# A hybrid DeltaNet and attention layer: inverses by rank-one updates on two engines, a bias table from 128 partitions, and new buffers in the second half

## The chip, the cores and the metric

The kernel runs on one core of a Trainium2 chip. A core has five engines that work side by side, each with its own instruction stream: TensorE (PE, matrix products into PSUM), VectorE (DVE), ScalarE (ACT), GpSimd (POOL) and SyncE (SP, which issues transfers). Transfers between DRAM and SBUF are issued from SP and from ACT and run on the core's DMA engines. The metric is the time of one execution on the device in microseconds; the median of three runs stands for a kernel. The profile comes from one more execution.

## The reference

The layer normalises x (2048 tokens by 1024), projects it by w_in, runs two token mixers side by side, and projects both back by w_out. This is its core, shortened:

```python
h = rms_norm(x, norm_w)
qkv_dn, z_dn, b_dn, a_dn, qkv_att, gate_att = split(h @ w_in)
# A: gated DeltaNet, 4 heads of 128, chunks of 64
q, k, v = split(silu(causal_depthwise_conv(qkv_dn, conv_w)))       # width 4
a_mat = tril_strict((beta * k) @ k.T * decay);  l_mat = a_mat + I   # per chunk, 64x64
u = solve(l_mat, beta * v);  w = solve(l_mat, beta * k * exp(gc))
# over the 32 chunks:  v_new = u - w @ S;  o = q_dec @ S + attn @ v_new
#                      S = S * g_last + k_tail.T @ v_new
y_dn = rms_norm(o) * silu(z_dn)
# B: dilated attention, 8 heads of 64, patterns (128,1), (512,4), (2048,16)
# scores + rel_bias[bucket(distance)], softmax; patterns weighed by their denominators
y_att = sum_p(weight_p * out_p) * silu(gate_att)
return x + concat(y_dn, y_att) @ w_out
```

All in float32. A large product is done as three: each operand is split into a high part (`wh`, `xh`, from ACT) and a low part (`wl`, `xl`, the remainder, from DVE), and high by high, low by high and high by low are summed in PSUM.

## The kernel before

Work stands in this order in the file, and a scheduler orders each engine's instructions by priorities (`tc.cur_priority`), so that the stages overlap.

1. **Projections of DeltaNet.** `conv_proj` (L460) makes q, k and v, 512 tokens by 128 channels at a time: 24 products `pj` (L206 to L208), scaled on DVE into `cu` (L474), the width-4 convolution as one ACT operation into `cy` (L476) and three DVE operations (L478), SiLU on ACT (L480) and a store to DRAM from ACT's queue (L481). `gate_proj` (L483) makes the attention's gate in the same manner. Their weights are 512 KB loads `wraw` (L187) into two buffers, split by ACT (L191) and DVE (L192).
2. **`stage1a`** (L501) forms the 64x64 matrices of the chunks (A) and the decays (E) and writes both to DRAM, in two halves of 16 chunks (`hf` 0 and 1).
3. **`inverse`** (L535) then inverts, per half, all 128 diagonal blocks of 32x32, one in each partition: the blocks come back from DRAM into `L`, ACT negates them, and for i = 1 to 31 DVE multiplies an i by i product (L545) and sums it along its rows into column i of `Tt` (L547). The inverse goes back over its place in A (L551), and a transposed copy goes to D (L552). Both writes, and later the loads of the weights, stand in SP's queue in the order of the schedule.
4. **Bias table** (L579 to L594): a one-hot product gives for 8 heads and 3 patterns a row of 256 biases, in 8 partitions. Three writes copy each row 64 times to `bs_d`, from which the attention later loads a skewed `bias` tile per head pair.
5. **`stage2`** (L606) prepares four chunks of a head pair: it loads kT, qT, vT, Qr, E, TT (A with its inverted blocks) and D0t (D) on SP's queue, and PE finishes the 64x64 inverse from the 32x32 blocks (L642), then forms the tiles of the delta rule (to L699). **`chain`** (L712) runs the rule chunk by chunk. **`dn_out`** (L741) loads `zs`, the gate of y_dn, scales and gates `o4` in place, and stores it to `y_d`. PE fills the time between with the projections of the attention (`proj_fill`, L886), whose operations carry the line L99, as do all that go through the file's helper.
6. **Attention and output projection.** From L1239 a table of steps (`at_step`, 12 steps to a head pair) calls a head pair's `load` (q, K, bias), `queries`, `keys`, `vload`, `scores`, `values` and its weighing by hand. `out_fill` (L1359) generates in the second half (steps from 48) the output projection's products `po`, that fill PE between them: `half_load` loads `yt` (y_dn) or `mt` (y_att), `half_split` splits it into `mh`, `wo_split` (L865) splits w_out, and `res_load` loads x or a stored partial sum into `res`. Buffers come from the pool `wo`, whose places are given out in the order of allocation.

## Time and profile before

| quantity | value |
|---|---|
| runs | 1434.2 us median of 3 (1432.68 to 1436.26) |
| profiled execution | 1434.53 us, of which the span of the trace is 1432.6 us |
| mean granted clock of PE | 0.988 |
| ACT busy | 47% of the span |
| DMA | 205.00 MB in 301154 packets, mean 143 GB/s |

The span is the time from the first to the last instruction in the trace; some 1.9 us of the execution lie around it. A row of a group names its line, engine, operation, tiles (out<-in), shape and count, then busy time and the mean of one in ns, and after the next bar the idle time of the engine just ahead of it and what ended that. A row of the timeline gives start, duration, engine and operation, with idle time and releaser in brackets. SPq and ACTq rows are issues of transfers. In the chain that ended last, a DMA row is the time in which a transfer was waited for.

### The profile page before, as it was taken

How to read it: one execution, taken by the hardware profiler on the slowest of the kernel's cores; microseconds unless marked ns; L12 is line 12 of the kernel's file. 1: busy time of each engine (PE TensorE's matmuls, PEld its weight loads, DVE VectorE, ACT ScalarE, POOL GpSimd, SP SyncE). 2: the span in 40 equal slices, each digit the busy share in tenths (PEclk: the TensorE clock that was granted, in tenths of full speed). 3: DMA queues.
4: the chain of work that ended last, by engine and by line, in shares of the span. 5: the costliest groups of instructions: out<-in, count | busy, mean ns of one | idle time of the engine just before them, and what ended most of it. 6: DMA issues, size and time to landing. Idle time of an engine off the chain costs nothing.

```text
span 1432.6 us, 28797 instructions
## 1 busy us (share of the span) xinstructions
PE 1376.4 (96%) x10262; PEld 1224.8 (85%) x10262; DVE 905.4 (63%) x2787; ACT 677.1 (47%) x1929; POOL 438.4 (31%) x507
## 2 busy tenths in 40 slices
PE   8999999999999997999999899999998989999998
PEld 7998777777777797999999889999997778888877
DVE  7535668799995365777777664634444645556465
ACT  5634436652221333444444376666565545555520
POOL 3000000000002113442332523565675275665500
PEclk9999999999999999999999999999999999999999
DMA  6563446763648646557553555274657474765664
GB/s 192 179 111 83 101 89 136 150 121 84 116 77 176 171 80 165 134 147 193 129 147 77 114 132 137 76 190 98 147 135 235 138 253 135 220 169 158 194 191 142
DMA packets 301154, 205.00 MB, mean 143 GB/s; under 512 B 149283, under 2 KB 271027, under 8 KB 300500
## 3 DMA queue, kind: packets, MB, share of 16 engines
q1 hardware_dynamic: 233924, 171.70, 48.6%
q10 hardware_dynamic: 67088, 31.47, 8.0%
q8 instruction: 81, 1.33, 0.4%
q14 instruction: 61, 0.50, 0.1%
HBM read 142.61 MB, written 60.50 MB: 142 GB/s over the span
## 4 chain that ended last, share of the span: by engine, by line
PE 66%; DVE 14%; DMA 9%; ACT 4%; issue 4%; SPq 1%; POOL 1%; ACTq 0%; DVEq 0%; POOLq 0%
PE pj L99 15%; PE po L99 9%; PE sc L99 6%; PE pz L99 5%; PE pv L99 4%; PE pj L206 4%; PE pj L207 4%; PE pj L208 4%; PE pt L99 4%; DVE cy L478 3%; DVE inv L545 2%; DMA kT<-cv 2%; PE C L719 2%; PE SU L725 2%; DVE inv L547 2%
## 5 line engine op out<-in xcount | busy, mean ns | idle before, releaser
L99 ACT ACTIVATE pr<-pr,ml 128x192 f32<-128x192 f32 (+2 forms) x384 | 156.8, 409 | 168.7 <-DVE ml L99 156.9
L99 PE MATMUL pj<-wh,xh 128*128 128x256 f32 (+1 forms) x776 | 228.2, 294 | 3.6 <-DVE t L99 2.3
L99 PE MATMUL pj<-wl,xh 128*128 128x256 f32 (+1 forms) x776 | 226.6, 292 | 0.0
L99 PE MATMUL pj<-wh,xl 128*128 128x256 f32 (+1 forms) x776 | 224.9, 290 | 0.0
L208 PE MATMUL pj<-xh,wl 128*128 128x512 f32 x512 | 203.6, 398 | 3.2 <-DVE wl L192 3.2
L206 PE MATMUL pj<-xh,wh 128*128 128x512 f32 x512 | 203.8, 398 | 1.4 <-ACT cy L480 1.2
L207 PE MATMUL pj<-xl,wh 128*128 128x512 f32 x512 | 203.0, 396 | 0.0
L99 PEld LDWEIGHTS pj<-wh,xh 128*128 128x128 f32 x776 | 147.6, 190 | 4.3 <-DVE t L99 2.7
L99 PEld LDWEIGHTS pj<-wl,xh 128*128 128x128 f32 x776 | 148.0, 191 | 0.6 <-issue 0.4
L99 PEld LDWEIGHTS pj<-wh,xl 128*128 128x128 f32 x776 | 147.7, 190 | 0.2
L99 DVE CUSTOM_DVE_ANT_0 pr<-sc,bias 128x192 f32<-128x192 f32 (+2 forms) x384 | 100.3, 307 | 74.3 <-PE sc L99 73.4
L208 PEld LDWEIGHTS pj<-xh,wl 128*128 128x128 f32 x512 | 96.5, 188 | 26.6 <-DVE wl L192 4.5
L206 PEld LDWEIGHTS pj<-xh,wh 128*128 128x128 f32 x512 | 96.6, 189 | 24.8 <-ACT cy L480 1.6
L478 DVE SCALAR_TENSOR_TENSOR cy<-cu,cw,cy 128x512 f32<-128x512 f32 x144 | 107.6, 749 | 15.9 <-ACT cy L476 14.4
L207 PEld LDWEIGHTS pj<-xl,wh 128*128 128x128 f32 x512 | 96.5, 188 | 22.0
L99 POOL COPY qz<-q 64x512 f32<-64x512 f32 x96 | 94.5, 984 | 57.8 <-PE sc L99 53.9
L662 POOL MEMSET at__4536<- 64x256 f32 x1 | 0.3, 306 | 354.5 <-PE pj L207 354.5
L99 DVE COPY pT<-pt 64x128 f32<-64x128 f32 (+2 forms) x220 | 69.4, 323 | 60.1 <-PE pt L99 56.8
L99 PE MATMUL po<-xh,mhh 128*128 128x512 f32 x212 | 89.6, 422 | 2.5 <-ACT mhh L99 2.5
L99 POOL TENSOR_TENSOR Fb<-Fb,op 128x256 f32<-128x256 f32 x84 | 70.6, 854 | 60.8 <-DMA Fb<-F 59.7
L99 PE MATMUL po<-xl,mhh 128*128 128x512 f32 x212 | 88.6, 418 | 0.0
L99 PE MATMUL po<-xh,mhl 128*128 128x512 f32 x212 | 88.4, 417 | 0.0
(365 smaller groups left out, 3169.8 us busy)
## 6 DMA issues: line engine op xcount, KB each, us to landing
wraw<-in_w_in SPq DMA_DIRECT2D x44, 512.0 KB, 7.0
cv<-cy ACTq DMA_DIRECT2D x48, 256.0 KB, 2.6
Fb<-F SPq DMA_DIRECT2D x64, 192.0 KB, 5.8
xr<-in_xT SPq DMA_DIRECT2D x32, 256.0 KB, 4.1
kT<-cv SPq DMA_DIRECT2D x32, 256.0 KB, 3.3
qk<-qs ACTq DMA_DIRECT2D x64, 128.0 KB, 3.6
res<-in_x SPq DMA_DIRECT2D x13, 512.0 KB, 5.3
V<-v_d SPq DMA_DIRECT2D x20, 256.0 KB, 6.2
```

Of the source, the lines that this page charges most:

```text
L99: i = f(*args, **kw)
L206: nc.tensor.matmul(ps, wh[:, k, c * P:(c + 1) * P], xh[tb][:, kt, :], start=kt == 0, stop=False)
L207: nc.tensor.matmul(ps, wh[:, k, c * P:(c + 1) * P], xl[tb][:, kt, :], start=False, stop=False)
L208: nc.tensor.matmul(ps, wl[:, k, c * P:(c + 1) * P], xh[tb][:, kt, :], start=False, stop=kt == KT - 1)
L478: nc.vector.scalar_tensor_tensor(y, u[:, i:i + 512], cw[:, ct, i:i + 1], y, op0=ALU.mult, op1=ALU.add)
L545: nc.vector.tensor_tensor(pr_[:, :i, :i], Tt[:, :i, :i], L[:, None, :i, i].to_broadcast([P, i, i]), op=ALU.mult)
L547: nc.vector.tensor_reduce(Tt[:, :i, i], pr_[:, :i, :i], axis=AX.X, op=ALU.add)
L662: nc.gpsimd.memset(at_[:CH, :, :CH], 0.0)
L719: nc.tensor.matmul(pc[:, s_], g["WQ"][:, u, s_], S0[:, s_], start=True, stop=True)
L725: nc.tensor.matmul(su[:, s_], g["Ks"][:, u, s_], VN, start=True, stop=True)
```

## The change

Of the whole diff (blank lines and unchanged parts are left out):

```diff
-    bs_d = dr.tile([8, 3, 64 * 256], F32, name="bs_d")
+    bs_d = dr.tile([3, 8, 64 * 256], F32, name="bs_d")
...
+        eng = (nc.vector, nc.gpsimd)[hf]
         nc.scalar.mul(L, L, -1.0)
-        nc.vector.memset(Tt, 0.0)
-        nc.vector.memset(Tt.rearrange("p c i -> p (c i)")[:, 0:1024:33], 1.0)
-        for i in range(1, 32):
-            nc.vector.tensor_tensor(pr_[:, :i, :i], Tt[:, :i, :i], L[:, None, :i, i].to_broadcast([P, i, i]),
-                                    op=ALU.mult)
-            nc.vector.tensor_reduce(Tt[:, :i, i], pr_[:, :i, :i], axis=AX.X, op=ALU.add)
+        eng.memset(Tt, 0.0)
+        eng.memset(Tt.rearrange("p c i -> p (c i)")[:, 0:1024:33], 1.0)
+        for j in range(31):
+            n, m = j + 1, 31 - j
+            eng.tensor_tensor(pr_[:, :n, :m], Tt[:, :n, j:j + 1].to_broadcast([P, n, m]),
+                              L[:, j:j + 1, n:].to_broadcast([P, n, m]), op=ALU.mult)
+            eng.tensor_tensor(Tt[:, :n, n:], Tt[:, :n, n:], pr_[:, :n, :m], op=ALU.add)
         D0 = pr_
-        nc.vector.tensor_copy(D0[:64], Tt[:64].rearrange("p c i -> p i c"))
+        eng.tensor_copy(D0[:64], Tt[:64].rearrange("p c i -> p i c"))
...
+    mid.tile([P, 512], F32, name="t0", bufs=2)
     rs0 = [mid.tile([P, 512], F32, name="big", bufs=3) for _ in range(2)]
...
+    rb16 = scr[:N_BUCKETS + 1, 1552:1680]
+    nc.vector.tensor_copy(rb16.rearrange("p (h c) -> p h c", h=8), rb[:, :, None].to_broadcast([N_BUCKETS + 1, 8, 16]))
+    bv = scr[:, :768].rearrange("p (a b) -> p a b", a=3)
...
-        nc.tensor.matmul(pb[:8, :n], rb, oh[:, i * 512:i * 512 + n], start=True, stop=True)
-    for i in range(3):
-        dma(dap(bs_d, i * 64 * 256, [[3 * 64 * 256, 8], [256, 64], [1, 256]]),
-            bv[:, i, None, :].to_broadcast([8, 64, 256]))
+        nc.tensor.matmul(pb[:, :n], rb16, oh[:, i * 512:i * 512 + n], start=True, stop=True)
+    def bias_out(i, after):
+        d = dma(dap(bs_d, i * 8 * 64 * 256, [[4 * 256, P], [256, 4], [1, 256]]),
+                bv[:, i, None, :].to_broadcast([P, 4, 256]))
+        tc.add_manual_dep(d.ins, after.ins.name, NOSYNC, reason="behind the loads of a group of chunks")
...
-    def stage2(pair, c0):
+    def stage2(pair, c0, dma2=dma):
...
-        dma(E, Es_d[hf][pair, cc:cc + 4].rearrange("u p i -> p u i"))
+        dma2(E, Es_d[hf][pair, cc:cc + 4].rearrange("u p i -> p u i"))
...
-            dma(TT[a:a + CH, :, a:a + CH], A_d[hf][pair, cc:cc + 4, a:a + CH].rearrange("u p i -> p u i"))
-            dma(D0[a:a + 32], dap(D0_d[hf], (m0 + s_) * 1024, [[32, 32], [2048, 4], [1, 32]]))
+            dma2(TT[a:a + CH, :, a:a + CH], A_d[hf][pair, cc:cc + 4, a:a + CH].rearrange("u p i -> p u i"))
+            dma2(D0[a:a + 32], dap(D0_d[hf], (m0 + s_) * 1024, [[32, 32], [2048, 4], [1, 32]]))
...
-        zs = dn.tile([P, 4, P], F32, name="zs", bufs=1)
+        zs = dn.tile([P, 4, P], F32, name="zs", bufs=2)
...
+            if c0 == 0:
+                tc.add_manual_dep(z.ins, last_D0[0].ins.name, NOSYNC, reason="behind the first preparations'")
...
-            nc.vector.scalar_tensor_tensor(g["o4"][:, u], g["o4"][:, u], f[:, 1, u:u + 1], zs[:, u],
+            nc.vector.scalar_tensor_tensor(zs[:, u], g["o4"][:, u], f[:, 1, u:u + 1], zs[:, u],
...
-                g["o4"][(1 - s_) * CH:(2 - s_) * CH])
+                zs[(1 - s_) * CH:(2 - s_) * CH])
...
-        G[p_] = at_prio("prep", stage2, p_, 0)
+        G[p_] = at_prio("prep", stage2, p_, 0, adma)
...
+        if c0 < 12:
+            at_prio("out", bias_out, c0 // 4, z)
...
     def w_out_load(k):
-        r = wp.tile([P, 4, 260], F32, name="wraw", bufs=2).rearrange("p a b -> p (a b)")[:, :1024]
+        if k == 2:
+            rs = [mid.tile([P, 512], F32, name="big", bufs=3) for _ in range(2)]
+        else:
+            rs = [wp.tile([P, 4, 260], F32, name="wraw", bufs=2).rearrange("p a b -> p (a b)")[:, :1024]]
...
-            at_step(b - 4, 1, g["load"])
+            at_step(*((b - 4, 1) if i < 4 else (b - 3, 0) if i == 4 else (b - 3, 2)), g["load"])
...
+    wo.tile([P, 512], F32, name="mt", bufs=2)
+    C1 = wo.tile([P, S], F32, name="C1")
+    loaded = {i: half_load(Q2[i], "dn", 4) for i in range(2)}
     RAW = [wo.tile([P, D], F32, name="res", bufs=3) for _ in range(2)]
-    C1 = wo.tile([P, S + 80], F32, name="C1")[:, :S]
-    loaded = {i: half_load(Q2[i], "dn", 4) for i in range(2)}
...
-        for k in range(4):
-            dma(RAW[k], w_out[(4 + k) * P:(5 + k) * P, :])
+        raws = {(0, 1): (raw_load, 0), (0, 2): (raw_load, 1), (0, 12): (raw_load, 2), (0, 22): (raw_load, 3)}
+        for k, at_ in enumerate(((0, 20), (1, 8), (1, 20), (2, 8))):
+            raws[at_] = (lambda k=k: wo_split(4 + k, RAW[k]),)
```

The inverse is now formed by 31 rank-one updates, of the first half on DVE and of the second on POOL. A step j multiplies column j of `Tt` by row j of `L` (a product of j + 1 by 31 - j) and adds it to the right. The bias table is laid out by pattern first, and each head's row stands in 16 partitions. Its three writes go one behind each of the first three groups of chunks. E, TT and D0t of the first two preparations go by ACT's queue (`adma`), the zs loads of the first group behind the last of these preparations' Qr loads. y_dn is written over `zs`, which has two buffers, instead of over `o4`. In the second half, the buffers of the pool `wo` are given out in another order (`mt`, `C1`, `yt`, `res`, `K1`), `mh` has one tile for both parts, w_out's third block is loaded early, into two `big` tiles that `wo_split` takes one by one, and its last four blocks are loaded and split at four places of the products each. The loads of q, K and bias of the head pair 4 stand two thirds of a step later (at the start of step b - 3), those of 5 to 7 at the end of that step.

SP's queue where the convolutions end and the second half's inverse comes back. `inv_2689` is L of the second half, loaded from `A1_71`; `A1_71<-inv`, `D01_75<-inv` are the writes of its result, `wraw` the weights of the gate, `big` the norms' rows. Before:

```order
L187 DMA wraw_3945<-in_w_in 128x4x256
L187 DMA wraw_4067<-in_w_in 128x4x256
L540 DMA inv_2689<-A1_71 64x32x32 x2
L551 DMA A0_70<-inv_2360 64x32x32 x2
L552 DMA D00_74<-inv_2361 64x1024
L187 DMA wraw_4073<-in_w_in 128x4x256
L187 DMA wraw_4204<-in_w_in 128x4x256
L187 DMA wraw_4210<-in_w_in 128x4x256
L187 DMA wraw_4332<-in_w_in 128x4x256
L551 DMA A1_71<-inv_2690 64x32x32 x2
L552 DMA D01_75<-inv_2691 64x1024
```

After:

```order
L540 DMA inv_2689<-A1_71 64x32x32 x2
L553 DMA A0_70<-inv_2360 64x32x32 x2
L554 DMA D00_74<-inv_2361 64x1024
L187 DMA wraw_3946<-in_w_in 128x4x256
L187 DMA wraw_4068<-in_w_in 128x4x256
L553 DMA A1_71<-inv_2690 64x32x32 x2
L554 DMA D01_75<-inv_2691 64x1024
L187 DMA wraw_4074<-in_w_in 128x4x256
L575 DMA big_3936<-rstd_d_69 128x512
L575 DMA big_3937<-rstd_d_69 128x512
L187 DMA wraw_4205<-in_w_in 128x4x256
L187 DMA wraw_4211<-in_w_in 128x4x256
```

The load of the blocks moved ahead of two weight loads, and the two writes of the result moved ahead of the four weight loads of the gate that they stood behind (`wraw_4073` is now `wraw_4074`).

SP's queue where the bias table is written (`bs_d`), among the loads of the second group's preparations. Before:

```order
L99 DMA wraw_7453<-in_w_in 128x4x256
L594 DMA bs_d_86<-K0_4460 8x64x256
L635 DMA TTz1_4474<-A0_70 64x4x64 x2
L636 DMA D0t_5102<-D00_74 32x4x32 x2
L594 DMA bs_d_86<-K0_4460 8x64x256 x2
L619 DMA qT_5089<-cv00_57 128x512
L629 DMA E2_5100<-Es0_72 128x4x64
L618 DMA kT_5088<-cv10_59 128x512
L620 DMA vT_4826<-cv21_62 128x512
```

After:

```order
L99 DMA wraw_7455<-in_w_in 128x4x256
L643 DMA TTz1_4473<-A0_70 64x4x64 x2
L601 DMA bs_d_86<-K0_4461 512x1x256
L644 DMA D0t_5102<-D00_74 32x4x32 x2
L627 DMA qT_5089<-cv00_57 128x512
L637 DMA E2_5100<-Es0_72 128x4x64
L626 DMA kT_5088<-cv10_59 128x512
L628 DMA vT_4825<-cv21_62 128x512
```

One of the three writes is left there, 512 rows from 128 partitions; the other two stand some 20 rows further on each.

SP's queue in the second half, at the loads of head pair 5 (`q1`, `K1`, `bias`) and of the next tile of x (`res<-in_x`). Before:

```order
L99 DMA V_13204<-v_d_84 128x4x128
L99 DMA q1_13237<-qk01_77 128x1024
L99 DMA K1_12654<-qk11_81 128x2048
L99 DMA bias_13240<-bs_d_86 64x3x192 x2
L99 DMA acc_d_104<-res_13001 128x1024
L99 DMA mx_d_103<-gt_13057 128x256
L99 DMA res_13318<-in_x 128x1024
L99 DMA V_13325<-v_d_84 128x4x128
```

After:

```order
L99 DMA V_13207<-v_d_84 128x4x128
L99 DMA acc_d_104<-res_13003 128x1024
L99 DMA mx_d_103<-gt_13061 128x256
L99 DMA res_13314<-in_x 128x1024
L99 DMA V_13321<-v_d_84 128x4x128
L99 DMA q1_13323<-qk01_77 128x1024
L99 DMA K1_12661<-qk11_81 128x2048
L99 DMA bias_13326<-bs_d_86 64x3x192 x2
```

The loads of q, K and bias moved behind the store of a partial sum, the load of x and a load of V.

More of the change, by code (lines that the diff above doesn't have):

```diff
@@ L780, in hybrid @@
         for p_ in range(2):
-            at_prio("out", dn_out, p_, c0, cur[p_])
+            z = at_prio("out", dn_out, p_, c0, cur[p_])
+        if c0 < 12:
+            at_prio("out", bias_out, c0 // 4, z)
     close(psD_g)
@@ L867, in wo_split @@
         if kt < 4:
-            nc.scalar.mul(wh, raw, dnw)
-            nc.vector.scalar_tensor_tensor(wl, raw, dnw, wh.bitcast(F32), op0=ALU.mult, op1=ALU.subtract)
+            for i, r in enumerate(raw):
+                n = r.shape[1]
+                h, l = wh[:, i * n:(i + 1) * n], wl[:, i * n:(i + 1) * n]
+                nc.scalar.mul(h, r, dnw)
+                nc.vector.scalar_tensor_tensor(l, r, dnw, h.bitcast(F32), op0=ALU.mult, op1=ALU.subtract)
         else:
@@ L881, in w_out_load @@
     def w_out_load(k):
-        r = wp.tile([P, 4, 260], F32, name="wraw", bufs=2).rearrange("p a b -> p (a b)")[:, :1024]
-        dma(r, w_out[k * P:(k + 1) * P, :])
-        return r
+        if k == 2:
+            rs = [mid.tile([P, 512], F32, name="big", bufs=3) for _ in range(2)]
+        else:
+            rs = [wp.tile([P, 4, 260], F32, name="wraw", bufs=2).rearrange("p a b -> p (a b)")[:, :1024]]
+        n = D // len(rs)
+        for i, r in enumerate(rs):
+            dma(r, w_out[k * P:(k + 1) * P, i * n:(i + 1) * n])
+        return rs
     def proj_fill():
@@ L917, in proj_fill @@
                     if o8 == 1:
-                        rs = [w_out_load(k) for k in range(2)]
+                        rs = [w_out_load(k) for k in range(3)]
                     if o8 == 4:
@@ L980, in load @@
                 dma(bias[s_ * CH:(s_ + 1) * CH],
[L981 removed]
+                    dap(bs_d, (2 * p + s_) * 64 * 256 + 63, [[255, CH], [8 * 64 * 256, 3], [1, 192]]))
             g["kc"] = {0: g["k1"].rearrange("p (c i) -> p c i", c=1)}
@@ L1312, in ring_mh @@
     def ring_mh():
-        return [wo.tile([P, 4, P], F32R, name="mh" + c, bufs=3) for c in "hl"]
+        t = wo.tile([P, 2, 4, P], F32R, name="mh", bufs=3)
+        return [t[:, 0], t[:, 1]]
     def res_load(tt, src, res=None):
@@ L1389, in split @@
                 if buf not in spare:
-                    t = wo.tile([P, S + (80 if buf == "C1" else 48)], F32R, name=buf)[:, :S]
+                    t = wo.tile([P, S + (0 if buf == "C1" else 150)], F32R, name=buf)[:, :S]
                     t = t.rearrange("p (a b k c) -> p a b k c", a=2, b=2, k=4)
@@ L1426, in out_fill @@
                     m += 1
-                    if nth < 2 and m in (8, 16):
-                        k = 2 * nth + m // 8 - 1
-                        wo_split(4 + k, RAW[k])
+                    if (nth, m) in raws:
+                        f, *args = raws.pop((nth, m))
+                        f(*args)
                     if m >= 3 * n and m % 3 == 0 and todo_:
```

20 lines of the change are left out of this document (11 added, 9 removed).

## The prediction, made before the changed kernel ran

> **What bounds the kernel now.** I read the page's first part, then the waits of PE, then windows with the granted clock.
>
> ```profile
> span 1432.6 us, 28797 instructions
> PE 1376.4 (96%) x10262; PEld 1224.8 (85%) x10262; DVE 905.4 (63%) x2787; ACT 677.1 (47%) x1929; POOL 438.4 (31%) x507
> ```
>
> PE is the bound. The change takes no matmul away, so all it can win lies in the 1432.6 - 1376.4 = 56.2 us in which PE is idle, and in what follows an idle stretch. The waits of PE (us in total, times, longest) say which those are:
>
> ```profile
> PE A L680 <- DMA vT<-cv: 6.6, 1, 6.6
> PE pv L99 <- DVE pT L99: 5.1, 2, 4.5
> PE sc L99 <- DVE ml L99: 4.3, 3, 2.3
> PE A L642 <- DMA D0t<-D: 4.2, 1, 4.2
> PE pv L99 <- DVE res L99: 3.7, 1, 3.7
> PE pj L208 <- DVE wl L192: 3.2, 3, 1.5
> PE po L99 <- DMA yt<-y_d: 1.8, 1, 1.8
> ...
> PE pj L206 <- ACT cy L480: 1.2, 1, 1.2
> ```
>
> A window behind the last-but-one of these (columns: stretch, length, PE, PEld, DVE, ACT, POOL busy with counts, granted clock, DMA share, GB/s) shows a second price:
>
> ```profile
> 1101.70:1105.10 3.40, 3.40 (x12) 3.21 (x11) 1.29 (x8) 1.26 (x5) 0.92 (x2) 0.50 0.54 188
> ```
>
> Behind the wait for yt (to 1099) the clock is 0.50 for 3.4 us. Work done in 3.4 us at half clock would take 1.7 us at full clock, so I put each wait of 1.8 us or more at its length and 1.6 us besides. By the Trainium skill (TensorE: Matmul & The Clock Gate, section Part 1: The HAM clock gate) the clock halves only after an idle window of about 3.4 us. The row has the half clock behind a wait of 1.8 us, so here the measurement decides. With that rule the term of yt below would be 1.6 us smaller, and nothing else would change.
>
> **The change part by part.**
>
> *Inverses, DVE's side.* They run beside the convolutions, where DVE is full:
>
> ```profile
> 324.00:360.00 36.00, 33.29 (x155) 26.06 (x154) 36.00 (x65) 9.52 (x14) 0.00 (x0) 1.00 0.33 68
> L545 DVE TENSOR_TENSOR inv<-inv 128x1 f32<-128x1 f32 (+30 forms) x62 | 48.6, 783 | 0.8 <-DMA D<-inv 0.2
> L547 DVE TENSOR_REDUCE inv<-inv 128x1 f32<-128x1 f32 (+30 forms) x62 | 31.1, 501 | 0.6
> L478 DVE SCALAR_TENSOR_TENSOR cy<-cu,cw,cy 128x512 f32<-128x512 f32 x30 | 22.2, 746 | 1.3 <-ACT cy L476 1.2
> L192 DVE TENSOR_TENSOR wl<-wraw,wh 128x1024 fp32r<-128x1024 f32 x2 | 2.4, 1217 | 0.0
> ```
>
> (The last two rows are of the window 345 to 400.) One inverse is (48.6 + 31.1) / 2 = 39.9 us of DVE now. The new form has 62 operations with 5456 products and 5456 sums instead of 10416 and 10416 elements, so at the same rates about 21 us; the second half's goes to POOL. DVE loses some 59 us of work between 279 and 443, and of the 3.2 + 1.2 us that PE waits there the 3.0 us before 360 should mostly go: 2.5 us.
>
> *Inverses, POOL's side.* POOL never runs such an operation in this trace. The nearest rows give its rate, and the rows after them what it shares with DVE:
>
> ```profile
> L99 POOL TENSOR_TENSOR gt<-gt,Fb 128x256 f32<-128x256 f32 x28 | 21.7, 776 | 2.2
> L99 POOL TENSOR_TENSOR ss<-ss,e 128x8 f32<-128x8 f32 x32 | 6.8, 212 | 182.6 <-DVE ss L99 160.1 <-DVE ml L99 22.2
> ...
> 921.46 0.74 POOL L99 TENSOR_TENSOR Fb<-Fb 128x256 f32<-128x256 f32 x1
> 922.16 1.87 POOL L99 TENSOR_TENSOR Fb<-Fb,op 128x256 f32<-128x256 f32 x1
> 921.52 1.76 DVE L99 TENSOR_TENSOR wl<-wraw,wh 128x1024 fp32r<-128x1024 f32 x1 [2.35 <-ACT wh L99]
> ```
>
> From 8 to 256 elements POOL goes from 212 to 776 ns: 2.27 ns an element and 0.19 us an operation. Alone it needs 62 x 0.19 + 10912 x 0.00227 = 36.8 us. But a POOL operation that starts at 922.16, while DVE subtracts two SBUF tensors until 923.28, takes 1.87 instead of 0.74 us: it stood still for those 1.1 us; and the subtraction took 1.76 instead of 1.22 us. So I take it that POOL and a DVE operation with two SBUF inputs shut each other out. In 345 to 400 DVE has (22.2 + 2.4) / 55 = 45% of such work, and POOL gets 55%. The Trainium skill (GPSIMD Engine Reference, section 1. Specifications) says that GpSimd shares its SBUF interfaces with VectorE and that DVE instructions with two SBUF inputs contend for them. The rows agree (1.87 us beside 0.74), and this speaks against the change; what comes out without any exclusion is the first rival.
>
> The load of the second half's blocks now stands right behind the last write of A, ahead of two weight loads:
>
> ```profile
> 338.60 0.36 SPq L531 DMA_DIRECT2D A<-t  x1
> 369.89 2.01 SPq L540 DMA_DIRECT2D inv<-A  x2
> 372.28 4.58 SPq L551 DMA_DIRECT2D A<-inv  x2
> 376.95 1.42 SPq L552 DMA_DIRECT2D D<-inv  x1
> 377.07 1.06 ACT L541 ACTIVATE inv<-inv 128x1024 f32<-128x1024 f32 x1 [2.83 <-DMA inv<-A]
> 404.01 28.48 SPq L187 DMA_DIRECT2D wraw<-in_w_in  x4
> wraw<-in_w_in SPq DMA_DIRECT2D x44, 512.0 KB, 7.0
> 428.04 0.50 PE L208 MATMUL pj<-xh,wl 128*128 128x512 f32 x1 [1.39 <-DVE wl L192]
> ```
>
> Load and negation took 377.07 + 1.06 - 369.89 = 8.2 us; behind a write of A at 338.6 and its landing POOL starts near 348. To 410, where the convolutions end, it does 62 x 0.55 = 34 us of its work, and the rest by 412.8. Then SP writes A and D (4.6 + 1.4 us; the copy for D stands beside the first) and only then loads the weights that it loaded at 404: issue 418.8, 7.0 us to land, 1.1 us on ACT (the negation's row, of the same size), 1.2 us on DVE: ready at 428.1. PE wants them where it stood at 428.04 - 1.39 = 426.6, now 2.5 us earlier: 424.1. So it waits 4.0 us and loses 1.6 us of clock where it waited 1.4: a **loss of 4.2 us**. Behind SP's writes also stand the next weight loads, and ACT's stores of the gate wait for them; three cy buffers cover ACT. If the inverse ends by 409, nothing is lost; each us behind that is one of PE's. Bounds: the 1.4 us won, or a wait of 18.6 + 1.6 us (second rival).
>
> *First preparations.* L642 (L650 in the changed file) waits for D0t, the last of the loads in SP's queue; the chain has
>
> ```profile
> 454.49 10.73 DMA kT<-cv
> 465.24 3.29 DMA D0t<-D
> ```
>
> E, TT and D0t now go by ACT's queue, beside kT, zs stands behind them, and A and D are written long before. The wait costs 4.2 + 1.6 us. PE now reaches the operation 14 matmuls earlier (155 of them took 33.3 us in the window from 324, so 3.0 us), and the load must land 3.0 + 4.2 us sooner; it is freed of the 10.73 us of kT. Between nothing and 5.8 I take 5.
>
> *Bias table.* SP issues (start, length):
>
> ```profile
> 512.11 0.29 SPq L594 DMA_DIRECT2D bs_d<-K  x1
> 517.55 6.23 SPq L636 DMA_DIRECT2D D0t<-D  x2
> ...
> 538.28 4.06 SPq L620 DMA_DIRECT2D vT<-cv  x1
> 546.24 1.10 SPq L636 DMA_DIRECT2D D0t<-D  x2
> ```
>
> An issue that takes 1.1 us at 546 takes 6.2 behind the writes from 8 partitions; vT is issued 26 us after the first write, and PE waits 6.6 + 1.6 = 8.2 us. The new writes read 128 partitions and stand apart by groups of chunks; a transfer of as many bytes to 128 partitions, the wraw row, lands in 7.0 us. I take 8; nothing would be won if the bytes alone held the queue.
>
> *Second half's start.*
>
> ```profile
> 1077.23 10.21 DMA bias<-bs_d
> 1087.52 0.38 ACTq L99
> 1095.68 3.24 DMA yt<-y_d
> ```
>
> ACT's store of v_d stands until the bias has landed; behind it xh, xl and pT are late, and pv waits 4.5 us. In the built program the store waits for the load of q instead, issued two places earlier. yt, issued at 1095.68 behind PE, may go when the bias is down, at 1087.5. So 4.5 + 1.6 and 1.8 + 1.6 us: 9.5, of which I take 8.5, since ACT's mhh (0.7 us) stays late.
>
> *Loads of later heads.*
>
> ```profile
> 1154.63 0.46 SPq L99 DMA_DIRECT2D q<-qk  x1
> 1158.48 9.59 DMA res<-in_x
> ```
>
> The load of res stood behind q, K and bias; now it stands ahead of them, 3.9 us earlier and with the queue clear. 3.7 + 1.6 = 5.3 us; I take 5. q comes later for POOL's qz, a bound of 2 us.
>
> *The rest.* The wait for ml at 1125 (2.3 + 1.6) keeps xl, mhl and res ahead of it on DVE; its order hardly changes: 1. Gating over z frees o4 sooner, off PE's path: 0. The splits of w_out keep their 1.1 us on ACT and 1.2 on DVE each (the rows of that size above) and stand further apart, beside PE's products; uncovered, one would cost those 2.3 us.
>
> **Sum.** 2.5 - 4.2 + 5 + 8 + 8.5 + 5 + 1 = 25.8 us. Moved queues bring waits that no row shows; I set two of 2.3 us, a middle wait of the list: 4.6. So 21.2 us off the profiled execution's 1434.5 (1.9 around the span) is 1413.3; the median, 1434.2, stands 0.3 lower: **1413**.
>
> **Rivals.** *POOL isn't shut out*: it ends at 385, nothing waits and the 1.4 us goes too: 4.2 + 1.4 better, 1407. For it: the operation at 921.46 ran its 0.74 us beside the subtraction; against it: the one behind stood.
>
> *POOL pays for strides.* DVE's products with strided operands take 783 ns for 10416 / 31 = 336 elements on average, 2.33 ns each against 746 / 512 = 1.46: 1.6 times. Were POOL's elements dearer likewise, the inverse would need 11.8 + 39.6 = 51.4 us and end at 427.4, and PE would wait 18.6 us instead of 4.0: 1428. Against it: the new operations read broadcast rows and columns, not the old column stride for each element.
>
> *Slower*: the same place at a higher price. 1438.5 is passed when the inverse ends 25.5 us later than forecast, at 438.3, that is from 62 us of POOL's own work, 1.7 times what its rows give. At twice (73.6 us) it ends at 449.6: 1450.
>
> *The waits move on.* The first preparations and the second half's start find the next late load: half of 5 + 8 + 8.5 is kept, 10.8 us worse: 1424. For it: these loads stand in one queue with many others; against it: the chain shows one late transfer at each place, and no other wait in the list is above 2.3 us.
>
> **Chances.** Forecast, 1405 to 1420: 0.55. Not shut out: 0.13. Strides: 0.13. Waits move on: 0.12. Slower: 0.07. The range from 1398 (every term at its upper end is 3.0 + 1.4 + 5.8 + 8.2 + 9.5 + 5.3 + 3.9 = 37.1 us, and not all of it is likely) to 1428 leaves out the slower case and the tails. A measurement here tells some 0.3% from no change, 1429.9 to 1438.5: faster 0.88, same 0.06, slower 0.06.
>
> **What would show it.** POOL operations of the inverse with 0.8 us where 128x8 rows have 0.2; its end near 413; a wait of pj for wl or wh near 424 of 4 us; L650 waiting under 2 us; no wait for vT; pv at the second half's start without a wait; SP issues behind bs_d under 1.2 us. I am wrong first if the inverse on POOL ends past 425 or before 409.

## The result, and the profile after

| | before | after |
|---|---|---|
| median, us | 1433.44 (4 runs, 1431.96 to 1436.26) | 1398.96 (4 runs, 1397.04 to 1401.44) |
| ratio, 95% interval | 1 | 0.976 [0.974, 0.978] |
| profiled execution, us | 1434.53 (span 1432.6) | 1397.04 (span 1395.2) |
| mean granted clock of PE | 0.988 | 0.997 |

The change saves 34.5 us by the medians and 37.4 us between the two profiled executions' spans. The profiled execution is the fastest of the four, so its trace shows a somewhat larger gain than the medians. The forecast was 1413: the sign and several of the mechanisms hold, but the gain is larger by some 14 us. The page of the changed kernel begins:

```profile
span 1395.2 us, 28823 instructions
...
PE 1362.5 (98%) x10262; PEld 1216.4 (87%) x10262; DVE 855.7 (61%) x2724; ACT 677.6 (49%) x1930; POOL 486.2 (35%) x572
```

The same 10262 matmuls take 1376.4 - 1362.5 = 13.9 us less, since fewer of them run at half clock, and PE's idle time falls from 56.2 to 1395.2 - 1362.5 = 32.7 us, by 23.5. The two add up to the 37.4 us. The waits of PE after the change (us in total, times, longest):

```profile
PE po L99 <- ACT mh L99: 4.2, 2, 2.5
PE sc L99 <- DVE ml L99: 3.5, 3, 1.4
...
PE A L650 <- DMA D0t<-D: 1.8, 1, 1.8
PE pt L99 <- ACT pT L99: 1.8, 1, 1.8
```

The waits for vT, res and yt are gone from the list, and D0t's has fallen from 4.2 to 1.8 us. The wait of `pt` for ACT's `pT` is new. That of `po` for ACT's `mh` is not: before, where the tile was called `mhh`, it stood at 2.5 us in two (longest 1.9), and it has grown to 4.2.

Where the time came from shows if the nth matmul of PE is compared with the nth matmul before. The starts are from both timelines, and the lead is before less after. Between numbers 1729 and 5404 the two kernels order some products differently, so that a lead there is good to about 1 us.

| matmul number (start after, us) | lead, us | what lies behind the gain since the row above |
|---|---|---|
| 1600 (265) | -0.2 | |
| 2400 (430) | 6.0 | convolutions beside the inverses: +6.2 |
| 2800 (502) | 11.0 | first preparations (D0t): +4.9 |
| 3400 (561) | 21.0 | no wait for vT behind the writes of the bias table: +10.0 |
| 7200 (976) | 23.6 | delta rule: +2.5 (gating over z, below) |
| 7400 (1000) | 25.1 | half clock behind a wait for `t`: +1.6 |
| 7800 (1045) | 23.1 | new wait of `pt` for `pT`: -2.0 |
| 8400 (1128) | 29.7 | start of the second half, and ml: +6.6 |
| 8600 (1154) | 35.3 | load of res: +5.5 |
| 10200 (1377) | 37.4 | a half-clock stretch at the end gone: +2.1 |

### The profile page after: what moved, and what is told of

Read it like the earlier page. It is cut to its first block, busy times and chain, and to the rows that moved or that the text cites. A ratio compares the mean times of both kernels' runs of the same rounds, so it can differ in the third digit from the quotient of the medians.

```text
span 1395.2 us, 28823 instructions
## 1 busy us (share of the span) xinstructions
PE 1362.5 (98%) x10262; PEld 1216.4 (87%) x10262; DVE 855.7 (61%) x2724; ACT 677.6 (49%) x1930; POOL 486.2 (35%) x572
## 4 chain that ended last, share of the span: by engine, by line
PE 80%; DVE 7%; DMA 4%; ACT 3%; POOL 2%; issue 2%; SPq 1%; ACTq 0%; DVEq 0%; POOLq 0%
PE pj L99 16%; PE po L99 10%; PE pj L207 7%; PE pj L208 7%; PE pj L206 7%; PE sc L99 7%; PE pz L99 6%; PE pv L99 4%; PE pt L99 4%; PE SU L733 2%; PE C L727 2%; ACT pr L99 1%; POOL Fb L99 1%; PE A L665 1%; PE pm L99 1%
## 5 line engine op out<-in xcount | busy, mean ns | idle before, releaser
L99 PE MATMUL po<-xh,mh 128*128 128x512 f32 x424 | 148.5, 413 | 5.3 <-ACT mh L99 4.2
L478 DVE SCALAR_TENSOR_TENSOR cy<-cu,cw,cy 128x512 f32<-128x512 f32 x144 | 112.1, 778 | 19.8 <-ACT cy L476 17.8
L99 PEld LDWEIGHTS po<-xh,mh 128*128 128x128 f32 x424 | 78.0, 189 | 19.4 <-ACT mh L99 4.8
L99 PE MATMUL po<-xl,mh 128*128 128x512 f32 x212 | 86.9, 410 | 0.0
```

The source lines that it names most:

```text
L99: i = f(*args, **kw)
L478: nc.vector.scalar_tensor_tensor(y, u[:, i:i + 512], cw[:, ct, i:i + 1], y, op0=ALU.mult, op1=ALU.add)
```

## The experiments

All are the changed kernel with one edit, unless the text says that they start from the kernel before. Each ratio is to the kernel before on the same chip. A difference to the changed kernel in microseconds compares medians from different runs and chips, on which the kernel before has medians from 1432.0 to 1434.1 us: it is good to some 2 us. No version clearly beat the changed kernel: of the two lowest medians, 1397.02 and 1397.95, the second lies within its own four runs and the first at their lower end, 1397.04.

### How fast POOL is, and what its end costs

In the changed kernel the second half's inverse occupies POOL from 355.3 to 403.7 us. Its two groups of operations (line, engine, names, count, busy time and mean ns of one), and the largest group of DVE in the same stretch (353 to 404 us):

```profile
L549 POOL TENSOR_TENSOR inv<-inv 128x31 f32<-128x31 f32 (+15 forms) x31 | 24.1, 776 | 2.4
L547 POOL TENSOR_TENSOR inv<-inv 128x31 f32<-128x31 f32 (+15 forms) x31 | 19.5, 631 | 3.2 <-DMA D<-inv 0.8
L478 DVE SCALAR_TENSOR_TENSOR cy<-cu,cw,cy 128x512 f32<-128x512 f32 x27 | 24.5, 908 | 4.6 <-ACT cy L476 3.9
```

The convolution's operation on DVE took 746 ns before, and here 908. What follows the inverse (SP's issues, then DVE's part of the split of the weights):

```profile
403.69 1.59 SPq L553 DMA_DIRECT2D A<-inv  x2
...
408.44 0.64 SPq L187 DMA_DIRECT2D wraw<-in_w_in  x1
...
418.11 1.23 DVE L192 TENSOR_TENSOR wl<-wraw,wh 128x1024 fp32r<-128x1024 f32 x1 [3.87 <-ACT wh L191]
```

The split ends at 418.11 + 1.23 = 419.34 us. Matching PE's matmuls one by one with the built order shows that the first product that reads these weights starts at 422.10. So the weights have 2.8 us to spare, and the wait of 4 us that the prediction put here does not exist.

**POOL's products issued twice**, to make the inverse late:

```diff
+            if hf:
+                eng.tensor_tensor(pr_[:, :n, :m], Tt[:, :n, j:j + 1].to_broadcast([P, n, m]),
+                                  L[:, j:j + 1, n:].to_broadcast([P, n, m]), op=ALU.mult)
             eng.tensor_tensor(Tt[:, :n, n:], Tt[:, :n, n:], pr_[:, :n, :m], op=ALU.add)
```

> The changed kernel with each of the 31 products of POOL's inverse issued twice (the same value again; the output is the reference's). In the changed kernel POOL's 62 operations ran from 355.3 to 403.7 beside the convolutions, and PE waited for nothing there. Theory A (POOL stands while DVE reads two SBUF tensors, and SP's queue holds the gate's weights behind the inverse's writes, as predicted): up to 404 POOL gets as far as before, the 31 further products need some 15 us, now without DVE's convolutions beside them, so their length falls back to 0.24 us for 31 elements and 0.65 us for 255; the inverse ends near 419, and past 409 each us is PE's: a wait for wl or wh of 8 to 12 us near 420, 1409 to 1413. Rival B (the place has much more slack than was predicted): no wait over 1 us there, 1398 to 1401.

Measured: 1404.26 us (1403.21 to 1405.87), 0.9796 [0.9777, 0.9816]. Three views of it (SP's issues; POOL's operations; a wait of PE):

```profile
397.14 2.71 SPq L187 DMA_DIRECT2D wraw<-in_w_in  x2
423.94 2.01 SPq L556 DMA_DIRECT2D A<-inv  x2
```
```profile
406.79 0.60 POOL L550 TENSOR_TENSOR inv<-inv 128x220 f32<-128x220 f32 x1
...
423.28 0.26 POOL L550 TENSOR_TENSOR inv<-inv 128x31 f32<-128x31 f32 x1
```
```profile
PE A L653 <- DMA D0t<-D: 4.0, 1, 4.0
```

Neither theory is met as it was written. The scheduler put the two weight loads ahead of A and D (397.14 against 423.94), so the weights had nothing to wait for, and the wait that the prediction feared could not be provoked. What a later inverse costs instead is the first preparations: the inverse ends 20.3 us later, PE waits 4.0 us for D0t in place of 1.8, and the clock is at half for 6.8 us, from 457.4. PE's loss is 4.5 us.

The run gives POOL's own speed. At 406.8 the convolutions are over, and an operation of 220 elements takes 0.60 us; at 423.3 one of 31 takes 0.26. That is 1.80 ns an element and 0.20 us an operation, and 62 x 0.20 + 10912 x 0.0018 = 32 us for one inverse alone. In the changed kernel, beside the convolutions, operations at that speed alternate with slower ones:

```profile
366.47 0.91 POOL L547 TENSOR_TENSOR inv<-inv 128x220 f32<-128x220 f32 x1
...
368.46 0.60 POOL L547 TENSOR_TENSOR inv<-inv 128x231 f32<-128x231 f32 x1
```

So the two engines do hold each other up: 0.91 for 0.60 us on POOL, and 908 for 746 ns on DVE. The inverse needed 48.4 us in place of 32, two thirds of POOL's own speed. The run with the doubled products also shows one such collision by itself, beside DVE's subtraction of two SBUF tensors:

```profile
417.00 1.39 DVE L192 TENSOR_TENSOR wl<-wraw,wh 128x1024 fp32r<-128x1024 f32 x1 [2.91 <-DMA gate<-cy]
417.39 1.23 POOL L547 TENSOR_TENSOR inv<-inv 128x112 f32<-128x112 f32 x1
418.70 0.37 POOL L550 TENSOR_TENSOR inv<-inv 128x112 f32<-128x112 f32 x1
```

POOL's operation takes 1.23 us where the next one of the same shape takes 0.37, and ends 0.23 us after the subtraction (418.62 against 418.39): it stood until DVE was done, as the prediction had read it from the kernel before.

**Both inverses on DVE**:

```diff
-        eng = (nc.vector, nc.gpsimd)[hf]
+        eng = nc.vector
```

> The changed kernel with both inverses on DVE, in the new form. Theory A (the rank-one form alone relieves DVE, POOL isn't needed): DVE was busy for 36 of the 72 us from 360 to 432, takes some 20 us more, the convolutions' operations fall back from 0.91 to 0.75 us each, and no wait of pj over 1 us comes: 1397 to 1401. Rival B (what counts is that DVE is free beside the convolutions): the waits of pj for cy and wl come back, 3 to 5 us before 440, 1402 to 1405.

Measured: 1398.85 us (1398.38 to 1399.27), 0.9757 [0.9736, 0.9778]: the same as with POOL. Groups of DVE between 250 and 412 us, and below them the convolution's operation in 345 to 404:

```profile
L547 DVE TENSOR_TENSOR inv<-inv 128x31 f32<-128x31 f32 (+15 forms) x62 | 20.9, 338 | 0.6
L549 DVE TENSOR_TENSOR inv<-inv 128x31 f32<-128x31 f32 (+15 forms) x62 | 20.8, 336 | 0.3
L478 DVE SCALAR_TENSOR_TENSOR cy<-cu,cw,cy 128x512 f32<-128x512 f32 x31 | 23.1, 747 | 0.8 <-ACT cy L476 0.6
```

Two inverses take 41.7 us, so one takes 20.9 where it took 39.9. The new form alone relieves DVE enough, and the second inverse is written back at 404.27 us, as early as from POOL (403.69). The move to POOL brings no time: DVE saves its 21 us of work, and part of that goes into operations that POOL slows down.

### The inverses and the first preparations

**The kernel before with the new inverses alone**: the part of the change at L535, with the first half on DVE and the second on POOL, and nothing else of it.

```diff
+        eng = (nc.vector, nc.gpsimd)[hf]
...
-        for i in range(1, 32):
+        for j in range(31):
+            n, m = j + 1, 31 - j
...
```

> The kernel before with the new inverses alone (rank-one updates, the second half's on POOL). Theory A (the inverses are worth what the trace of the changed kernel shows up to 436, where PE was 6 us ahead, and this is kept): PE stays 5 to 8 us ahead to the end, 1426 to 1429. Rival B (the lead is lost at the first preparations, whose loads stand on SP's queue for as long as before): the wait for D0t grows from 4.2 to 8 us or more, 1432 to 1435. Rival C (the inverse on POOL also takes A's and D's writes out of that queue's way, so that the wait for D0t gets shorter as well): the wait falls below 3 us, 1422 to 1426.

Measured: 1417.4 us (1416.75 to 1420.46), 0.9891 [0.9871, 0.9912], a gain of 16.7 us, beyond what any of the three gave; the short wait for D0t is the sign that Rival C named. SP's issue of kT for the first preparations, and that wait of PE:

```profile
446.45 1.10 SPq L620 DMA_DIRECT2D kT<-cv  x1
```
```profile
PE A L644 <- DMA D0t<-D: 1.3, 1, 1.3
```

kT is issued at 446.45 where it was at 454.49, and D0t at 456.58 where it was at 465.24, on the same queue in the same order. PE's lead is 6.0 us at matmul 2400, as in the full change, and 11.5 at 2600. The inverses alone bring what the prediction had put down, for the most part, to the loads' move to ACT's queue.

**The first loads back on SP's queue**:

```diff
-        G[p_] = at_prio("prep", stage2, p_, 0, adma)
+        G[p_] = at_prio("prep", stage2, p_, 0)
```

> The changed kernel with E, TT and D0t of the first two preparations on SP's queue again. The run of the inverses alone had a wait of only 1.3 us for D0t with these loads on SP's queue and zs ahead of them. Theory A (what shortened that wait was the earlier inverse, whose writes had held SP's queue; the queue of the loads counts for nothing): the wait stays at 1 to 3 us, 1397 to 1401. Rival B (ACT's queue is what brought them forward, as the prediction had it): D0t waits 4 us or more with the half clock behind it, 1402 to 1406.

Measured: 1397.02 us (1396.34 to 1397.46), 0.9757 [0.9734, 0.978]. Nothing is lost. The wait for D0t, 1.8 us in the changed kernel, is down to 0.6 in two, and PE is some 1 us earlier there. ACT's queue was not the cause.

**The old inverses in the changed kernel**:

```diff
-        eng = (nc.vector, nc.gpsimd)[hf]
...
-            eng.tensor_tensor(pr_[:, :n, :m], Tt[:, :n, j:j + 1].to_broadcast([P, n, m]),
-                              L[:, j:j + 1, n:].to_broadcast([P, n, m]), op=ALU.mult)
-            eng.tensor_tensor(Tt[:, :n, n:], Tt[:, :n, n:], pr_[:, :n, :m], op=ALU.add)
+            nc.vector.tensor_tensor(pr_[:, :i, :i], Tt[:, :i, :i], L[:, None, :i, i].to_broadcast([P, i, i]),
+                                    op=ALU.mult)
+            nc.vector.tensor_reduce(Tt[:, :i, i], pr_[:, :i, :i], axis=AX.X, op=ALU.add)
...
```

> The changed kernel with the old inverses, both on DVE by rows. Alone the new inverses gave 16.7 us. Theory A (two parts stand in for each other: the first preparations' loads on ACT's queue and zs behind them do without SP's queue, which the late inverse holds to 448, so only what PE gained beside the convolutions is lost, some 6 us): 1404 to 1408, with a wait for D0t under 2.5 us. Rival B (the gains add up, so taking the inverses out costs what putting them in brought): 1412 to 1417, with a wait for D0t or kT of 4 us or more and the half clock behind it.

Measured: 1411.91 us (1408.65 to 1413.65), 0.9866 [0.9829, 0.9902], 13 us slower than the changed kernel: what the inverses bring, they bring in the finished kernel too. PE lies 7.8 us behind by matmul 2400 and 13.9 from 2600 on. The wait, ACT's issue of E, and the chain that ended last, in that stretch:

```profile
PE A L648 <- DMA D0t<-D: 3.8, 1, 3.8
```
```profile
452.17 0.45 ACTq L635 DMA_DIRECT2D E<-Es  x1
```
```profile
452.91 6.41 DMA wraw<-in_w_in
459.34 0.67 ACTq L641
...
460.05 7.90 DMA D0t<-D
```

On ACT's queue the loads are late all the same. Between its issues of E (452.17) and TT (L641, 459.34) ACT does nothing; by the chain, TT's issue waits until a load of weights has landed, which SP issued at 452.91, behind the late inverse's writes (444.72 to 449.71). In the changed kernel the same load is issued at 440.64 and TT at 446.60. In the trace, TT's issue waits on the semaphore that this transfer raises and that TT's own transfer raises next; why the two share it is not shown.

**The kernel before with the second half's writes on ACT's queue**:

```diff
-            dma(dap(A_d[hf], b * (32 * CH + 32), ...), Tt[b * 64:(b + 1) * 64])
-        dma(D0_d[hf].rearrange("m i c -> m (i c)"), ...)
+            (dma, adma)[hf](dap(A_d[hf], b * (32 * CH + 32), ...), Tt[b * 64:(b + 1) * 64])
+        (dma, adma)[hf](D0_d[hf].rearrange("m i c -> m (i c)"), ...)
```

> The kernel before, with one difference: the second half's writes of A and D are issued from ACT's queue, so that SP goes on with the loads of the first preparations while DVE still inverts. Theory A (the wait for D0t comes from SP's queue standing at these writes to 448): the wait falls from 4.2 to 2.5 us or less, PE gains 3 to 6 us there, 1426 to 1430. Rival B (the loads wait for buffers that come free with PE's last gate products, at 447.6, whatever SP does): the wait stays within 1 us of 4.2, 1431 to 1435.

Measured: 1434.11 us in 10 runs, 1.0015 [0.9997, 1.0034]. The wait for D0t stays at 4.7 us, which is Rival B's result. This doesn't separate the queue from the inverse cleanly, because the writes now hold up ACT's split of the weights (at 450.03 us), on which SP's next loads depend: the block moved with the writes. It agrees with the four runs above, in which the time of the inverse's end decides and not the queue.

### The bias table

**The table from 8 partitions again**, as in the kernel before:

```diff
-        nc.tensor.matmul(pb[:, :n], rb16, oh[:, i * 512:i * 512 + n], start=True, stop=True)
+        nc.tensor.matmul(pb[:8, :n], rb, oh[:, i * 512:i * 512 + n], start=True, stop=True)
...
+    for i in range(3):
+        dma(dap(bs_d, i * 64 * 256, [[3 * 64 * 256, 8], [256, 64], [1, 256]]),
+            bv[:, i, None, :].to_broadcast([8, 64, 256]))
```

> The changed kernel with the old bias table: 8 partitions, three writes together, the old layout; all else as changed. Theory A (the writes from 8 partitions hold SP's queue, and the preparation behind them is late): issues behind them take 4 to 6 us, PE waits 6 to 8 us for vT near 525, 1405 to 1410. Rival B (the earlier first preparations and ACT's queue had already taken the preparation out of their way): a wait under 2 us, 1398 to 1401.

Measured: 1409.21 us (1406.24 to 1410.2), 0.9827 [0.9806, 0.9847], 10.3 us slower. In the trace PE falls behind by 9.3 us between matmuls 2800 and 3400. The wait is back, and the clock is at half for 6.8 us, from 536.1, during the wait:

```profile
PE A L683 <- DMA vT<-cv: 4.7, 1, 4.7
```

SP's issues beside the table's writes, in this run and then in the changed kernel:

```profile
503.00 0.91 SPq L597 DMA_DIRECT2D bs_d<-K  x2
504.34 9.00 SPq L639 DMA_DIRECT2D D0t<-D  x2
```
```profile
502.05 0.56 SPq L601 DMA_DIRECT2D bs_d<-K  x1
503.38 1.20 SPq L644 DMA_DIRECT2D D0t<-D  x2
```

Behind the new write a pair of D0t issues takes 1.20 us, and the next pair (at 521.12) 1.96, where a pair took 9.00 here and 6.23 in the kernel before. The run undoes the partitions, the layout and the spreading of the writes together. In the kernel before the slow issues begin behind the first single write already, which speaks for the partitions, but the parts were not separated.

### The second half

**The loads of the heads at their old steps**:

```diff
-            at_step(*((b - 4, 1) if i < 4 else (b - 3, 0) if i == 4 else (b - 3, 2)), g["load"])
+            at_step(b - 4, 1, g["load"])
```

> The changed kernel with the loads of q, K and bias of the last four head pairs at their old steps. Theory A (these loads ahead of res made PE wait 3.7 us for res near 1165, with the half clock behind it): the wait for res is back, PE falls behind by 5 to 6 us between 1120 and 1160, 1403 to 1406; the wait for ACT's store near 1070 may come back as well, then 1406 to 1410. Rival B (the new buffers alone take the collision away): no wait over 1.5 us for res, 1398 to 1401.

Measured: 1405.16 us (1398.11 to 1406.14), 0.9804 [0.9771, 0.9837]. The wait of `pv` at the start of the second half comes back, 2.7 us in place of 0.4:

```profile
1069.21 1.12 PE L99 MATMUL pv<-pT,V 128*64 128x128 f32 x8 [2.69 <-DVE pT L99]
```

The wait for res comes back too, but small, 1.0 us in place of the 3.7 of the kernel before:

```profile
PE pv L99 <- DVE res L99: 1.0, 1, 1.0
```

So the step of the fifth head's load is part of the gain at the start of the second half, and the steps of the later loads are worth little against the wait for res. The interval touches that of the changed kernel, and one of the four runs, 1398.11, lies within those of the changed kernel. In the trace PE falls behind by 7.7 us, of which 3.0 lie before the second half: the size, some 5 us, is less sure than the place.

**The buffers in their old order**, and then **the buffers and the splits of w_out at their old places**. The first undoes the allocation (`mh`, `C1`, `mt`, and what follows); the second undoes besides:

```diff
-        raws = {(0, 1): (raw_load, 0), (0, 2): (raw_load, 1), (0, 12): (raw_load, 2), (0, 22): (raw_load, 3)}
-        for k, at_ in enumerate(((0, 20), (1, 8), (1, 20), (2, 8))):
-            raws[at_] = (lambda k=k: wo_split(4 + k, RAW[k]),)
...
+                    if nth < 2 and m in (8, 16):
+                        k = 2 * nth + m // 8 - 1
+                        wo_split(4 + k, RAW[k])
```

> The changed kernel with the old order and sizes of the second half's buffers (res, C1, yt, K1, two mh tiles), the loads and splits of w_out spread as changed. Theory A (the order of the buffers decides when yt may be loaded, as the prediction had it for 1.8 + 1.6 us): yt is issued behind PE's last projection, PE waits 1.5 to 2.5 us for it, 1400 to 1404. Rival B (the buffers don't decide, the spread splits and the load of q did it): no wait for yt, 1398 to 1400.

> As the run before it, and also the loads of w_out's last four blocks together at the start and their splits at the old places. Theory A (the splits at the old places collide with the weighing on DVE and ACT, which cost the 2.3 + 1.6 us for ml near 1125): 3 to 5 us more than the run with the old buffer order alone. Rival B (the splits' place is free): within 1.5 us of that run.

Measured: 1397.95 us (1395.12 to 1400.43), 0.9763 [0.9736, 0.9791], for the first: the new places of the buffers bring nothing, and yt is waited for in neither kernel, as Rival B had it. For the second, 1403.58 us (1401.23 to 1407.34), 0.9798 [0.9767, 0.9828]: spreading the loads and splits is worth some 5.6 us; the runs of the two don't overlap, their intervals do. What comes back is a wait for ml and one for V, each with 3.4 us at half clock (waits of PE), and a wait for yt of 0.9 us:

```profile
PE sc L99 <- DVE ml L99: 4.3, 3, 2.3
...
PE sc L99 <- DMA V<-v_d: 2.1, 1, 2.1
```

No wait for res comes back here. With both the loads' steps and the splits old, in the run of the inverses alone, where the buffers are old too, PE waits 2.9 us for it; with the old steps alone (the run above) 1.0, with the old splits 0. The new steps alone take that wait away, and the spread splits alone most of it.

### Gating over z

**Gating in place over o4, with one buffer for zs**:

```diff
-        zs = dn.tile([P, 4, P], F32, name="zs", bufs=2)
+        zs = dn.tile([P, 4, P], F32, name="zs", bufs=1)
...
-            nc.vector.scalar_tensor_tensor(zs[:, u], g["o4"][:, u], f[:, 1, u:u + 1], zs[:, u],
+            nc.vector.scalar_tensor_tensor(g["o4"][:, u], g["o4"][:, u], f[:, 1, u:u + 1], zs[:, u],
```

> The changed kernel with the gated output written over o4 again and one zs buffer. In the trace of the changed kernel PE gains 2.5 us between 580 and 800 that the prediction put at nothing. Theory A (o4 and zs, which stand until y_d is written, held the delta rule's stores back): the delta rule's stage takes 2 to 4 us longer, 1400 to 1403. Rival B (the gain there comes from loads that stand in another order on SP's queue): within 1 us, 1397.5 to 1400.

Measured: 1400.98 us (1398.63 to 1405.16), 0.9795 [0.9758, 0.9832]: the runs overlap those of the changed kernel, so the time alone decides nothing. In the trace PE falls behind by 3.0 us between matmuls 2600 and 5400. The view of the tile o4 (printed as o) lists until when the engine sat idle ahead of its operations (us, times); in the kernel before, and then in this one, it has the store of y_d among them:

```profile
  DMA y_d<-o: 13.4, 5
```
```profile
  DMA y_d<-o: 9.9, 3
```

It is ACT's copy into o4 (L742) that waits: with gating in place the buffer is free only when its store has landed. In the changed kernel this wait does not occur. Most of it is hidden from PE, but not all.

**Four parts alone** on the kernel before: rank-one inverses (both on DVE), the table, the loads' steps and the spread splits. Left as before are SP's queue for the first loads, one zs, gating in place, and the buffers, which had cost nothing, or little, when undone one by one. (w_out's third block stays early, in its two `big` tiles, and both inverses in the new form are on DVE.)

```diff
+        eng = nc.vector
...
+            at_step(*((b - 4, 1) if i < 4 else (b - 3, 0) if i == 4 else (b - 3, 2)), g["load"])
...
         zs = dn.tile([P, 4, P], F32, name="zs", bufs=1)
...
             nc.vector.scalar_tensor_tensor(g["o4"][:, u], g["o4"][:, u], f[:, 1, u:u + 1], zs[:, u],
```

> The changed kernel without five of its edits: both inverses on DVE, the first preparations' loads on SP's queue and zs not held behind them, one zs buffer with the output gated over o4, the old order of the second half's buffers and two mh tiles. What is left of the change: the rank-one form, the table from 128 partitions with its three writes apart, the steps of the loads, and the spread loads and splits of w_out. Theory A (these four carry the gain, since the runs without one of the other edits lost nothing): 1397 to 1401. Rival B (the edits stand in for each other, and without all of them a wait comes back): 1402 to 1408.

Measured: 1408.74 us (1406.01 to 1411.07), 0.9852 [0.9811, 0.9892]: 9.8 us short of the changed kernel. PE lies 1.1 us behind it at matmul 3200 and 11.9 at 5500, so the loss lies in the delta rule. The chain that ended last, PE's row, and a window (length, PE, PEld, DVE, ACT, POOL busy, granted clock, DMA share, GB/s) at one such place:

```profile
772.86 6.00 DMA y_d<-o
```
```profile
780.23 1.20 PE L727 MATMUL C<-S,WQ 128*128 128x128 f32 x4 [3.64 <-DVE S L737]
```
```profile
775.10:785.30 10.20, 6.56 (x30) 6.01 (x29) 4.87 (x18) 2.41 (x11) 0.00 (x0) 0.50 0.24 61
```

The store of the gated o4 is waited for 6.0 us. ACT's copy into that buffer stands, DVE's addition behind it stands 4.0 us (at 779.24), the state S behind that is late, and PE waits 3.6 us, to 780.23; around that wait the clock is at half for 10.2 us. That is the edit which the prediction had priced at nothing. How much of the 9.8 us is the gating and how much the single zs (for whose load DVE waits in this kernel too, 9.8 us in three waits) was not separated. Nor is it shown why the same edit costs 3.0 us of PE's lead when it is undone alone and some 10 here: which of the other parts covers the wait stays open.

## Why the prediction was right, and where it was wrong

| step | forecast, us | measured, PE's lead, us |
|---|---|---|
| inverses beside the convolutions (2.5 - 4.2) | -1.7 | +6.2 |
| first preparations | 5 | +4.9 |
| bias table | 8 | +10.0 |
| gating over z | 0 | +2.5 in the stage of the delta rule |
| second half's start, and ml | 8.5 + 1 | +6.6 |
| loads of later heads | 5 | +5.5 |
| new waits | -4.6 | -2.0 |
| half clock not priced (at 1000 and at the end) | 0 | +1.6 + 2.1 |
| sum | 21.2 | 37.4 |

The time of 1398.96 us lies inside the stated range, 1398 to 1428, by 1 us, and outside the forecast's own 1405 to 1420. The rival of a POOL that isn't held up (1407) did not come true either. That the 37.4 us in the traces equal the 37.1 of the sum of the upper ends is chance, since the parts differ, as the table shows.

**The step that failed most is the loss of 4.2 us behind POOL.** The deadline was nearly right, and POOL's duration was wrong. The forecast had 36.8 us of POOL's own work at 55% speed, done at 412.8. The runs show 32 us at two thirds, done at 403.7, with a start 7 us later than forecast. By the prediction's own rule (nothing is lost if the inverse ends by 409) no wait was due, and an end before 409 was one of its signs of being wrong. PE wanted the weights at 422.1, not 424.1, because its lead there was larger than the 2.5 us allowed for; so the true deadline lay at about 403.7 + 2.8 = 406.5. The rate came from 128x8 and 128x256 rows of other kinds of operands, and that line was too steep: 2.27 ns an element in place of 1.80.

That POOL and DVE hold each other up was right. The Trainium skill (GPSIMD Engine Reference, section 1. Specifications) names such contention without a size; here it made POOL's 0.60 us into 0.91 and DVE's 746 ns into 908.

**DVE's side was right in kind and too small.** One inverse takes 20.9 us on DVE, as forecast (21). Windows of the changed kernel show how full DVE still is:

```profile
324.00:360.00 36.00, 36.00 (x157) 29.17 (x156) 32.02 (x79) 12.28 (x17) 5.15 (x12) 1.00 0.69 117
360.00:396.00 36.00, 36.00 (x157) 29.12 (x156) 24.78 (x34) 9.66 (x14) 32.71 (x43) 1.00 0.29 64
```

PE is busy for all of 324 to 360, where it was for 33.29 us. Over the whole stage PE waits 1.0 us (0.7 for wl, 0.3 for kT) where it had waited 5.8; the forecast counted 3.0 of these, took the 1.4 at 428 as lost and left out kT. The other 1.4 us of the +6.2 are shorter matmul time, which no term had.

**First preparations: the size was right by luck and the cause mostly wrong.** The prediction gave it to ACT's queue, to zs and to the earlier writes of A and D together. With the loads back on SP nothing is lost, with the new inverses alone the gain is there, and with the old inverses it goes. The earlier end of the inverse is the cause; it lets the same loads go some 8 us earlier on SP's queue. The size came out by two errors. Windows over the same 200 matmuls before and after:

```profile
436.30:482.10 45.80, 41.43 (x201) 33.00 (x200) 19.62 (x29) 10.64 (x18) 12.20 (x24) 0.93 0.75 182
```
```profile
430.20:470.10 39.90, 38.12 (x202) 30.78 (x201) 11.06 (x23) 9.91 (x17) 10.98 (x22) 1.00 0.70 170
```

The wait fell by only 2.4 us (4.2 to 1.8), and the matmul time by 3.3, since before it 6.8 us at half clock lay there, where the prediction had put 1.6 us for the clock. Some 1 us of this is gone again by matmul 2800.

**Bias table and later heads: right**, in mechanism and within 2 us. That the table is worth some 10 us was shown by undoing it; a wait of 1.0 us for `tmp`, at 556.3 before, goes with it and was in no term. For res the prediction named the loads' steps; the spread of the splits alone takes most of that wait away as well.

**Second half's start: one part holds, one failed.** The later step of the fifth head's load removes the wait of `pv` (4.47 us before, 0.38 after), as forecast: PE gains 5.6 us there, of the 6.1 in the sum. The yt part, 1.8 + 1.6 us, gave nothing. yt is no longer waited for, but the product behind it also needs ACT's split of yt (`mhh`, now `mh`). Before, PE waited 1.78 us for yt and 0.68 for the split; after, it waits 2.45 us for the split alone. PE's rows after the change, the first of the new wait for `pT`, the second of this one:

```profile
1037.19 0.55 PE L99 MATMUL pt<-cs,pr 128*128 128x128 f32 x3 [1.77 <-ACT pT L99]
1072.24 0.50 PE L99 MATMUL po<-xh,mh 128*128 128x512 f32 x1 [2.45 <-ACT mh L99]
```

Before, the two waits were followed by 3.4 us at half clock from 1101.7; after, the one is followed by 3.4 us of it from 1073.3. So the prediction, which left mhh at 0.7 us, took away a wait with another right behind it. What fills the +6.6 instead is ml, 2.5 us where 1 was forecast; a wait of 0.8 us for `mh` at 1113 takes some 1 us back. The two waits of 2.3 us that the prediction set without a place can be read as this one and the 1.77 us for `pT`.

**Gating over z: the step "off PE's path: 0" failed.** It was 2.5 us in the changed kernel. The chain of the kernel before already went through this store, twice:

```profile
636.07 5.92 DMA y_d<-o
...
739.43 5.60 DMA y_d<-o
```

In the kernel with four parts the same wait stands on PE's path and costs more.

**The clock.** The prediction put 1.6 us on each wait of 1.8 us or more. It took this from one row behind yt, ahead of which two waits stood, of 1.78 and 0.68 us. To see the spread, one wait of PE, for `t`, can be compared over all kernels, since it stands in each. PE's row in the changed kernel, then a window with the granted clock third from the end in the changed kernel, in the kernel before and in the one with the old buffers, where the wait of 2.21 us ends at 993.92 and the half clock begins within it:

```profile
992.70 0.39 PE L99 MATMUL pj<-wh,xh 128*128 128x256 f32 x1 [2.29 <-DVE t L99]
```
```profile
992.70:996.10 3.40, 3.40 (x35) 3.10 (x36) 1.71 (x11) 2.49 (x10) 2.09 (x5) 1.00 0.86 223
```
```profile
1016.30:1019.70 3.40, 3.40 (x19) 3.18 (x21) 1.19 (x9) 2.60 (x10) 2.09 (x5) 0.51 1.03 175
```
```profile
993.20:1000.00 6.80, 6.08 (x34) 5.53 (x35) 2.50 (x12) 3.71 (x13) 5.43 (x7) 0.50 0.68 179
```

One wait of 2.2 to 2.3 us comes with no half clock, with 3.4 us of it, or with 6.8. By PE's lead from matmul 7300 to 7400 that costs 0, 1.5 or 2.7 us. The value of 1.6 was the middle of what occurs, but a single place can't be forecast by it. It may also be part of why single runs of one kernel differ: the four of the changed kernel, 1397.04 to 1401.44 us, have granted clocks from 0.997 down to 0.995.

## What to carry to other kernels

Ask of each late transfer which work's end released it before crediting a queue: the same loads came in time on two queues once the inverse ended earlier, and late on both when it did not. Before pricing the end of a wait, look for the next one behind it: yt came in time, and PE waited as long for `mh`. An operation moved to POOL is not free while DVE works on two SBUF operands, so halve its work on DVE first and see whether the move is still needed. Edits that cost little or nothing when undone one by one can cost 10 us when undone together, so measure the reduced kernel before calling the rest needless.
